# Stick-breaking attention on one core: where the running product over the keys is scanned

## The chip, the core and the metric

The kernel runs on one core of one Trainium2 chip. The metric is device time in microseconds (us), taken over the whole program. Its engines are named as the profile names them: PE (TensorE matmuls), PEld (its weight loads), DVE (VectorE), ACT (ScalarE), POOL (GpSimd) and SP (SyncE, which issues the DMAs).

## What is computed

One layer of a streaming encoder with two token mixers side by side: branch A is a differential softmax attention, branch B a stick-breaking attention. The input is one prompt of 2048 tokens of width 1024 and eight short samples of 16 tokens each with 512 cached keys. Branch B has 8 heads of 64. Cut to branch B, the reference is:

```python
def stick_breaking_attention(q, k, v, qpos, kpos):
    z = einsum('bqhd,bkhd->bhqk', q, k) * (HEAD_DIM_B ** -0.5)
    mask = kpos[None, :] < qpos[:, None]
    log_1m = where(mask, log_sigmoid(-z), 0.0)
    log_a = log_sigmoid(z) + cumsum(log_1m, axis=3, reverse=True) - log_1m
    a = where(mask, exp(log_a), 0.0)
    return einsum('bhqk,bkhd->bqhd', a, v)
```

Without logarithms: the weight of a key is sigmoid(z) of that key times the product of sigmoid(-z) over all later keys. The product over later keys is a running product from the last key to the first, and the kernel computes it with a scan instruction along the keys.

## The kernel before

The work goes by units and query tiles. A unit is one pair of heads of one branch; units 0, 2, 4, 6 are of branch A, units 1, 3, 5, 7 of branch B. In each unit the kernel goes through 16 query tiles of 128 tokens (and one tile with the samples' tokens, first). For each tile it projects queries, keys and values (PE, L428), then scores the tile against all keys up to it, then turns the scores into weights, and two tiles later (`PV_LAG`) multiplies the weights with the values (PE, L700 and L701). Tile t has t+1 blocks of 128 keys, so the last tiles of a unit are the longest. The instruction streams of projection, scores and values are woven into each other by `interleave`, and projections run ahead by about five tiles (`LEAD`), so the last score tiles of a unit stand beside the first projections of the next. Each engine works through its own queue in program order.

For one head of branch B and one tile the steps are these:

- The scores come in chunks of up to 512 keys, each in one PSUM bank of the tag "s", of which there are three. PE writes a chunk with two matmuls (L639, L640), and the last one of a tile gets a mask by a third (L643). Chunks are taken from the last key to the first.
- `evacuate` runs two ACT instructions for each chunk: sigmoid(z) goes to SBUF, into the buffer `sc_p` (L562), and then sigmoid(-z) goes back into the same PSUM bank (L563). Both are recorded under line L119, that of the helper `act`; the masked keys have a score so low that sigmoid(-z) is 1 and sigmoid(z) is 0.
- `stick` scans the chunk on DVE (L616), from its last key to its first, out of PSUM into the SBUF buffer `sc_n`. The second operand is a column of zeros in SBUF, `zero_t`, broadcast along the keys, so that each step computes state times data plus 0. The start value is a constant (2 to the 14th) for the last chunk of all and otherwise the last value of the chunk before, a column of `sc_n`.
- A segment is up to 1024 keys (`SEG` = 8 blocks), and has one buffer `sc_p` and one `sc_n`, six of each. Where a later segment exists, its first column is copied beside the segment's end first (L615).
- When a segment is done, `stick_weights` multiplies sigmoid(z) with the running product of the next key on POOL (L622), both in SBUF. `turn` then splits the weights in a high and a low half in 16 bits: a cast on ACT (L572) and a subtraction on DVE (L573), both from SBUF to SBUF, and SP issues a transposing DMA (L580) that makes the operand `wt` of the value matmuls.

POOL also turns branch A's queries and keys by their positions (L469, L471, L474), multiplies branch B's output with its gate path (L683), and takes part of the splitting of weights (L292). DVE also splits queries, keys and values of the projections (L295, L463) and evacuates branch A's scores (L558).

The samples' scores (`scores_all`, L776 to L781) use the same helpers, with 128 new keys and 512 cached keys in one segment of 640.

Of the kernel before, what the change touches and what calls it, by code (L numbers as in the profile page):

```python
# [20 lines left out]
AF = mybir.ActivationFunctionType  # L21
# [4 lines left out]
P = 128  # L26
# [83 lines left out]
def layer_kernel(ctx: ExitStack, tc: tile.TileContext, a: dict):  # L110
    nc = tc.nc
    V, S, G, T = nc.vector, nc.scalar, nc.gpsimd, nc.tensor
# [4 lines left out]
    def act(**kw):  # L117

        i = S.activation(**kw)  # L119
        if last_table[0] is not None:  # L120
            tc.add_manual_dep(i.ins, last_table[0].ins.name, NOSYNC, reason="table order")
        last_table[0] = i
        return i
# [63 lines left out]
    def bank(tag, dt=F32):  # L187
        return ps.tile([P, 512 if dt == F32 else 1024], dt, tag=tag, name=f"ps_{tag}", bufs=BANKS[tag])
# [16 lines left out]
    zero_t = con.tile([P, 1], F32, name="zero_t")  # L205
# [330 lines left out]
    def new_job(U, t, c, nb, pool=None):  # L536

        segs = [(0, nb)] if t == NT else [(lo, min(lo + SEG, nb)) for lo in range(0, nb, SEG)]
        return dict(U=U, t=t, c=c, pool=pool, segs=[dict(lo=lo, hi=hi) for lo, hi in segs])

    def buffers(job, seg):
        if "p" not in seg:
            for x in "pn":
                if job["t"] == NT:
                    seg[x] = job["pool"].tile([P, 5 * P], F32, tag="dsc", name="dsc", bufs=4)
                else:
                    seg[x] = scp.tile([P, SEG * P + 4], F32, tag=x, name="sc_" + x, bufs=SC_BUFS)

    def evacuate(job, seg, c, p, lo, n, sc_pos, sc_neg, ch):

        buffers(job, seg)
        if job["U"]["kind"] == 0:
            if "mx" not in job:
                job["mx"] = tiny.tile([P, 2, 4], F32, tag="mx", name="mx")
                job["nch"] = 0
            job["nch"] = max(job["nch"], ch + 1)
            dst = seg[("p", "n")[c]]
            V.tensor_scalar(out=dst[:, lo : lo + n], in0=p[:, 0:n], scalar1=sc_pos, scalar2=None,  # L558
                            op0=ALU.mult, op1=ALU.max, accum_out=job["mx"][:, c, ch : ch + 1])
        else:  # L560

            act(out=seg["p"][:, lo : lo + n], in_=p[:, 0:n], func=AF.Sigmoid, scale=sc_pos)  # L562
            act(out=p[:, 0:n], in_=p[:, 0:n], func=AF.Sigmoid, scale=sc_neg)  # L563

    def turn(job, seg, scale=None):

# [36 lines left out]
            V.scalar_tensor_tensor(out=p, in0=n, scalar=r[:, 2:3], in1=p, op0=ALU.mult, op1=ALU.add)  # L603
            turn(job, seg, r[:, 0:1])

    def stick(seg, later, lo, n, src):

        nk = (seg["hi"] - seg["lo"]) * P
        dst = seg["n"]
        if lo + n == nk and later is None:  # L610
            first = 2.0 ** STICK
        else:
            first = dst[:, lo + n : lo + n + 1]
            if lo + n == nk:
                V.tensor_copy(out=first, in_=later["n"][:, 0:1])  # L615
        V.tensor_tensor_scan(out=dst[:, lo : lo + n][:, ::-1], data0=src[:, 0:n][:, ::-1], data1=zero_t[:, 0:1].to_broadcast([P, n]),  # L616
                             initial=first, op0=ALU.mult, op1=ALU.add)

    def stick_weights(job, seg, later):
        m = (seg["hi"] - seg["lo"]) * P - (later is None)  # L620
        p, n = seg["p"], seg["n"]
        G.tensor_tensor(out=p[:, 0:m], in0=p[:, 0:m], in1=n[:, 1 : m + 1], op=ALU.mult)  # L622
        turn(job, seg)

    def scores(U, t, jobs):

        sc, kind = U["sc"], U["kind"]
        nch = t // 4 + 1
        own = [new_job(U, t, c, t + 1) for c in range(1 + kind)]
        jobs += own  # L630

        def chunk(c, ch):
            job = own[c if kind == 1 else 0]
            seg = job["segs"][ch * 4 // SEG]
            n = 512 if ch < t // 4 else (t % 4 + 1) * P
            p = bank("s")
            qst, kk = U["q", t], U["k"][ch]
            diag = ch == t // 4
            T.matmul(p[:, 0:n], qst[:, c, :], kk[:, c, 0:n], start=True, stop=False)  # L639
            T.matmul(p[:, 0:n], qst[:, 2 + c, :], kk[:, c, 0:n], start=False, stop=not diag)  # L640
            if diag:
                m = mask_a if kind == 0 else mask_b
                T.matmul(p[:, n - m.shape[1] : n], idb, m, start=False, stop=True)  # L643
            evacuate(job, seg, c, p, ch * 512 - seg["lo"] * P, n, sc[:, 3:4], sc[:, 4:5], ch)
            if kind == 0:
                if diag and c == 1:
                    softmax_pair(job)
                return
            i = job["segs"].index(seg)
            later = job["segs"][i + 1] if i + 1 < len(job["segs"]) else None  # L650
            stick(seg, later, ch * 512 - seg["lo"] * P, n, p)
            if ch * 4 == seg["lo"]:
                if later is not None:
                    stick_weights(job, later, None)
                if i == 0:
                    stick_weights(job, seg, later)

        def silu():

            z = silu_z[t % len(rings)]  # L660
            sg = stg.tile([P, 256], F32, tag="r2", name="r2", bufs=1)[:, 0:P]
            act(out=sg, in_=z, func=AF.Sigmoid)
            V.tensor_tensor(out=z, in0=z, in1=sg, op=ALU.mult)

        order = [(c, ch) for ch in range(nch) for c in range(2)] if kind == 0 else \
                [(c, ch) for c in range(2) for ch in reversed(range(nch))]
        return ([(0.1, silu)] if kind == 1 else []) + [(2.0 if ch < t // 4 else (t % 4 + 1) / 2, lambda c=c, ch=ch: chunk(c, ch)) for c, ch in order]

    def natural(U, t, po, pool=stg):
# [52 lines left out]
    def sample(U, dec, qpad, cs):  # L722
# [33 lines left out]
        def scores_all():  # L756

            box["jobs"] = [new_job(U, t, c, 5, dec) for c in range(heads)]
            qsam, kn = box["s"][:, 0:4, :], box["s"][:, 4:6, :]
            mask = mask_as if kind == 0 else mask_bs  # L760
            pn = bank("s")
            for c in range(2):
                p = pn[:, c * P : (c + 1) * P]
                T.matmul(p, qsam[:, c, :], kn[:, c, 0:P], start=True, stop=False)
                T.matmul(p, qsam[:, 2 + c, :], kn[:, c, 0:P], start=False, stop=False)
                T.matmul(p, idb, mask, start=False, stop=True)
            for c in range(2):
                pc = bank("s")
                for b in range(2):
                    for f in range(2):  # L770
                        for i in range(4):
                            T.matmul(pc[i * 32 : i * 32 + 32, :], qpad[:, f * 2 + c, 2 * i + b, :], box["k", i][:, b * 4 : b * 4 + 4, c, :],
                                     start=(b == 0 and f == 0), stop=(b == 1 and f == 1))
                job = box["jobs"][c % heads]
                seg = job["segs"][0]
                evacuate(job, seg, c, pn[:, c * P : (c + 1) * P], 512, P, sc[:, 3:4], sc[:, 4:5], 1)  # L776
                evacuate(job, seg, c, pc, 0, 512, box["f"][:, 0:1], box["f"][:, 1:2], 0)
                if kind == 1:
                    stick(seg, None, 512, P, pn[:, c * P : (c + 1) * P])
                    stick(seg, None, 0, 512, pc)  # L780
                    stick_weights(job, seg, None)  # L781
            if kind == 0:
                softmax_pair(box["jobs"][0])
# [39 lines left out]
        steps = [[] for _ in range(13)]  # L823
        steps[4] += [one(queries)]
        steps[6] += [one(scores_all)]
        for i in range(4):
            steps[1 + i] += [one(keys, i)]
# [596 lines left out]
```

## Time and profile before

| what | value |
|---|---|
| median of 3 runs | 2347.12 us (2343.01 to 2352.8) |
| the profiled execution's own time | 2352.01 us |
| its span, from the first to the last instruction | 2350.2 us |
| mean granted TensorE clock in it | 0.965 |

Durations of instructions are those of the profiled execution; its own time is a little above the median of the three runs, and its span is 1.8 us shorter than its time. A row of a group of instructions gives line, engine, operation, the tiles written and read, shape and count, then busy time in us and the mean of one in ns, then the idle time of the engine just before them and who ended it. A row of the timeline gives start and duration in us; rows of the waits give who waited for whom, the sum in us, the count and the longest. `ps_s` is a PSUM bank of scores, `dsc` the samples' buffer in place of `sc_p` and `sc_n`.

### The profile page before, as it was taken

What the parts mean: (1) busy time and instruction counts of PE and PEld (TensorE: products, weight loads), DVE (VectorE), ACT (ScalarE), POOL (GpSimd) and SP (SyncE); (2) the same over time, 40 slices, a digit from 0 to 9 for tenths busy, and PEclk for the clock granted to TensorE, in tenths of its full rate; (3) what the DMA queues carried; (4) which work ended last, traced back from release to release, by engine and by line L of the source; (5) the groups of instructions that cost most, each with busy time, mean ns of one, the idle gap of its engine ahead of it and who ended that gap; (6) DMA issues with size and microseconds to landing.
All of it is one profiled execution on the core that took longest, in us unless ns stands there. A gap on an engine that the chain in (4) does not pass through costs nothing. (4 is left out here: it accounts for less than half of the span.)

```text
span 2350.2 us, 42700 instructions
## 1 busy us (share of the span) xinstructions
PE 2124.9 (90%) x15272; PEld 1144.5 (49%) x15272; DVE 1725.1 (73%) x3652; ACT 1644.4 (70%) x3260; POOL 705.0 (30%) x610
## 2 busy tenths in 40 slices
PE   5898899998999999899999979998996879988998
PEld 3554454444555445445545545554553344544443
DVE  4848866779875667978667797877688877777663
ACT  4557878787886778878677777866777656665541
POOL 1533012446300334731033474103335111221111
PEclk8999899999999999999999999999996989999999
DMA  9766759887895988867577787766687999999531
GB/s 334 252 203 177 165 127 263 180 188 163 207 227 131 213 199 189 175 175 191 139 188 175 186 171 185 192 146 149 142 175 162 288 238 250 237 249 243 157 103 48
DMA packets 834357, 445.34 MB, mean 189 GB/s; under 512 B 537210, under 2 KB 777130, under 8 KB 833632
## 3 DMA queue, kind: packets, MB, share of 16 engines
q1 hardware_dynamic: 833196, 442.24, 76.5%
q8 instruction: 119, 1.95, 0.3%
q14 instruction: 94, 0.77, 0.1%
q10 hardware_dynamic: 948, 0.39, 0.1%
HBM read 245.60 MB, written 69.24 MB: 134 GB/s over the span
## 5 line engine op out<-in xcount | busy, mean ns | idle before, releaser
L622 POOL TENSOR_TENSOR sc_p<-sc_p,sc_n 128x127 f32<-128x127 f32 (+7 forms) x192 | 314.2, 1640 | 834.8 <-DVE sc_n L616 812.5
L428 PE MATMUL ps_mm<-wb,hs 128*128 128x512 f16 x1632 | 412.1, 380 | 5.1 <-DMA hs<-hT_d 3.0
L428 PEld LDWEIGHTS <-hs 128*128 128x128 f16 x3120 | 275.8, 99 | 264.5 <-issue 14.8
L428 PE MATMUL ps_mm<-wa,hs 128*128 128x512 f16 x1488 | 377.7, 384 | 9.0 <-DVE qbuf L463 3.8
L616 DVE TENSOR_TENSOR_SCAN sc_n<-ps_s,sc_n,zero_t 128x512 f32<-128x512 f32 x192 | 245.5, 1279 | 80.8 <-ACT ps_s L119 77.5
L639 PE MATMUL ps_s<-k,qst 128*128 128x512 f16 (+3 forms) x640 | 227.5, 356 | 37.2 <-DVE sc_n L616 25.8
L573 DVE TENSOR_TENSOR sc_n<-sc_p,sc_n 128x128 f16<-128x128 f32 (+7 forms) x192 | 211.5, 1106 | 51.8 <-ACT sc_n L572 51.3
L504 PEld LDWEIGHTS <-hs 128*128 128x128 f16 x1632 | 155.6, 98 | 181.4 <-DVE qst L532 5.5
L119 ACT ACTIVATE sc_p<-ps_s,usc 128x512 f32<-128x512 f32 (+3 forms) x320 | 204.3, 638 | 35.3 <-PE ps_s L640 27.9
L640 PE MATMUL ps_s<-k,qst 128*128 128x512 f16 (+3 forms) x640 | 227.1, 356 | 0.0
L572 ACT CAST sc_n<-sc_p 128x128 f16<-128x128 f32 (+7 forms) x192 | 154.9, 811 | 78.9 <-POOL sc_p L622 76.0
L700 PE MATMUL ps_o<-v,wt 128*128 128x128 f16 x1088 | 172.2, 226 | 35.1 <-DMA wt<-sc_n 35.1
L119 ACT ACTIVATE ps_s<-ps_s,usc 128x512 f32<-128x512 f32 (+3 forms) x328 | 199.4, 608 | 0.0
L504 PE MATMUL ps_t<-wb,hs 128*128 128x512 f16 x816 | 192.9, 380 | 2.5 <-DVE qst L532 2.2
L504 PE MATMUL ps_t<-wa,hs 128*128 128x512 f16 x816 | 192.3, 381 | 3.1 <-DVE qst L532 2.2
L1341 PE MATMUL ps_o<-wo,wb 128*128 128x512 f16 x816 | 189.2, 386 | 4.0 <-ACT wb L1163 4.0
L701 PE MATMUL ps_o<-v,wt 128*128 128x64 f16 x1088 | 158.3, 198 | 0.0
L700 PEld LDWEIGHTS <-wt 128*128 128x128 f16 x1088 | 105.6, 101 | 100.1 <-DMA wt<-sc_n 46.4
L558 DVE TENSOR_SCALAR_CACHE_REDUCE sc_n<-ps_s,usc 128x512 f32<-128x512 f32 (+3 forms) x160 | 106.5, 666 | 42.2 <-PE ps_s L640 22.9
L616 DVE TENSOR_TENSOR_SCAN sc_n<-ps_s,zero_t 128x128 f32<-128x128 f32 (+3 forms) x128 | 104.2, 815 | 41.0 <-ACT ps_s L119 38.0
L558 DVE TENSOR_SCALAR_CACHE_REDUCE sc_p<-ps_s,usc 128x512 f32<-128x512 f32 (+3 forms) x160 | 106.4, 665 | 35.6 <-PE ps_s L640 26.1
L701 PEld LDWEIGHTS <-wt 128*128 128x128 f16 x1088 | 103.4, 101 | 54.5 <-issue 1.9
(358 smaller groups left out, 4531.3 us busy)
## 6 DMA issues: line engine op xcount, KB each, us to landing
hs<-hT_d SPq DMA_DIRECT2D x130, 512.0 KB, 4.4
g_d<-gt SPq DMA_DIRECT2D x68, 256.0 KB, 4.4
wb<-g_d SPq DMA_DIRECT2D x26, 512.0 KB, 5.7
out_dram<-pr SPq DMA_DIRECT2D x204, 64.0 KB, 2.4
o_d<-o SPq DMA_DIRECT2D x136, 64.0 KB, 2.0
hs<-o_d SPq DMA_DIRECT2D x17, 512.0 KB, 5.1
out_dram<-x SPq DMA_DIRECT2D x17, 512.0 KB, 2.8
wide<-in_w_ada_dram SPq DMA_DIRECT2D x8, 1024.0 KB, 7.8
```

Source lines behind the costliest of these rows:

```text
L119: i = S.activation(**kw)
L428: T.matmul(box["p"], box["h"][:, hi, k, :], U["w"][k][:, wi, :], start=(n == 0), stop=(n == 3 * KT - 1))
L504: T.matmul(box["g"][:, 0:gw], box["h"][:, hi, k, :], U["wg"][k // per][:, k % per, wi, :], start=(j == 0), stop=(j == 3 * KT - 1))
L558: V.tensor_scalar(out=dst[:, lo : lo + n], in0=p[:, 0:n], scalar1=sc_pos, scalar2=None, op0=ALU.mult, op1=ALU.max, accum_out=job["mx"][:, ...
L573: V.tensor_tensor(out=lo, in0=src, in1=hi, op=ALU.subtract)
L616: V.tensor_tensor_scan(out=dst[:, lo : lo + n][:, ::-1], data0=src[:, 0:n][:, ::-1], data1=zero_t[:, 0:1].to_broadcast([P, n]), initial=fi ...
L622: G.tensor_tensor(out=p[:, 0:m], in0=p[:, 0:m], in1=n[:, 1 : m + 1], op=ALU.mult)
L639: T.matmul(p[:, 0:n], qst[:, c, :], kk[:, c, 0:n], start=True, stop=False)
L640: T.matmul(p[:, 0:n], qst[:, 2 + c, :], kk[:, c, 0:n], start=False, stop=not diag)
L700: T.matmul(po[:, c * P : (c + 1) * P], wt[:, wj, :], vt[:, c, :, :], start=first, stop=False)
L701: T.matmul(po[:, c * P : c * P + 64], wt[:, nb + wj, :], vt[:, c, 0, :], start=False, stop=last)
L1341: T.matmul(po, st["y"][:, yi * 8 + k, :], wo[j * 4 + k // 2][:, wi, k % 2, :], start=(n == 0), stop=(n == 3 * KT - 1))
```

## The change

sigmoid(-z) is written to SBUF, into `sc_n`, instead of back into the PSUM bank, and it is written before sigmoid(z). The scan no longer follows each chunk: it runs once for a whole segment, in place in `sc_n`, when the segment's last chunk (the one with its first keys) has been evacuated. For the samples the two scans of 128 and 512 keys become one of 640. The copy of the later segment's first column, the multiplication on POOL and all that follows stay.

```diff
@@ evacuate
+            act(out=seg["n"][:, lo : lo + n], in_=p[:, 0:n], func=AF.Sigmoid, scale=sc_neg)
             act(out=seg["p"][:, lo : lo + n], in_=p[:, 0:n], func=AF.Sigmoid, scale=sc_pos)
-            act(out=p[:, 0:n], in_=p[:, 0:n], func=AF.Sigmoid, scale=sc_neg)
@@ stick
-    def stick(seg, later, lo, n, src):
+    def stick(seg, later, lo, n):
...
-        V.tensor_tensor_scan(out=dst[:, lo : lo + n][:, ::-1], data0=src[:, 0:n][:, ::-1], data1=zero_t[:, 0:1].to_broadcast([P, n]),
+        x = dst[:, lo : lo + n][:, ::-1]
+        V.tensor_tensor_scan(out=x, data0=x, data1=zero_t[:, 0:1].to_broadcast([P, n]),
                              initial=first, op0=ALU.mult, op1=ALU.add)
@@ scores, chunk
-            stick(seg, later, ch * 512 - seg["lo"] * P, n, p)
             if ch * 4 == seg["lo"]:
+                stick(seg, later, 0, (seg["hi"] - seg["lo"]) * P)
                 if later is not None:
                     stick_weights(job, later, None)
@@ sample, scores_all
-                    stick(seg, None, 512, P, pn[:, c * P : (c + 1) * P])
-                    stick(seg, None, 0, 512, pc)
+                    stick(seg, None, 0, 5 * P)
                     stick_weights(job, seg, None)
```

## The prediction, made before the changed kernel was run

> **What bounds the kernel now.** I read the page's busy shares first, then busy time by stretch of 50 us, then the scan line by itself, then waits and timeline where the stretches differ.
>
> ```profile
> span 2350.2 us, 42700 instructions
> PE 2124.9 (90%) x15272; PEld 1144.5 (49%) x15272; DVE 1725.1 (73%) x3652; ACT 1644.4 (70%) x3260; POOL 705.0 (30%) x610
> 850.00:900.00 50.00, 49.10 (x318) 25.24 (x316) 38.94 (x59) 37.35 (x74) 19.54 (x14) 1.00 0.69 154
> 500.00:550.00 50.00, 41.45 (x320) 22.19 (x319) 45.89 (x54) 43.41 (x80) 33.73 (x25) 1.00 0.93 186
> 950.00:1000.00 50.00, 42.05 (x373) 24.01 (x371) 48.74 (x75) 38.62 (x77) 34.37 (x27) 0.97 0.88 168
> 1350.00:1400.00 50.00, 39.73 (x340) 22.33 (x340) 48.25 (x50) 41.25 (x78) 37.08 (x27) 1.00 0.86 185
> 1750.00:1800.00 50.00, 33.26 (x291) 19.43 (x289) 46.18 (x57) 41.06 (x72) 29.54 (x17) 0.76 0.82 166
> sum 200.00, PE 156.49 PEld 87.95 DVE 189.06 ACT 164.35 POOL 134.71; mean PE 39.12 PEld 21.99 DVE 47.26 ACT 41.09 POOL 33.68
> ```
>
> The columns of a stretch are length, then PE, PEld, DVE, ACT and POOL busy, granted clock, DMA share, GB/s. The whole kernel is PE's (90%), and so is the middle of a branch-B unit: 49.10 of 50 us in 850:900, with DVE at 38.94. The four last stretches, one at the end of each branch-B unit, differ: DVE has 189.06 of 200 us, PE only 156.49. There the last, longest query tiles meet the next unit's first projections, and DVE sets the pace. So the change is decided by what it does to DVE in these four places; elsewhere DVE has room.
>
> How much of DVE is scan, by shape, and what stands beside it:
>
> ```profile
> L616 DVE TENSOR_TENSOR_SCAN sc_n<-ps_s,sc_n,zero_t 128x512 f32<-128x512 f32 x192 | 245.5, 1279 | 80.8 <-ACT ps_s L119 77.5
> L616 DVE TENSOR_TENSOR_SCAN sc_n<-ps_s,zero_t 128x512 f32<-128x512 f32 x32 | 38.9, 1215 | 9.4 <-ACT ps_s L119 8.3 <-DMA wb<-in_cache_b_k_dram 1.1
> L616 DVE TENSOR_TENSOR_SCAN sc_n<-ps_s,zero_t 128x384 f32<-128x384 f32 x32 | 30.4, 950 | 12.9 <-ACT ps_s L119 11.7 <-PE ps_s L643 1.2
> L616 DVE TENSOR_TENSOR_SCAN sc_n<-ps_s,zero_t 128x256 f32<-128x256 f32 x32 | 21.9, 683 | 14.1 <-ACT ps_s L119 13.5 <-PE ps_t L521 0.4
> L616 DVE TENSOR_TENSOR_SCAN sc_n<-ps_s,zero_t 128x128 f32<-128x128 f32 x32 | 13.1, 411 | 4.6 <-ACT ps_s L119 4.5
> L616 DVE TENSOR_TENSOR_SCAN sc_n<-ps_s,sc_n,zero_t x192: 1265/1282/1285, 353.5 to 1801.2; 128x512 f32<-128x512 f32 x192
> L573 DVE TENSOR_TENSOR sc_n<-sc_p,sc_n x192: 266/1093/3052, 331.5 to 1808.3; 128x1024 f16<-128x1024 f32 x80, 128x128 f16<-128x128 f32 x16, 128x256 f16<-128x256 f32 x16, 128x384 f16<-128x384 f32 x16
> ```
>
> Of line and durations (minimum/median/maximum in ns): 192 scans of one shape all lie between 1265 and 1285. The subtraction L573, whose two inputs are both in SBUF, goes to 3052. The timeline of one tail says why:
>
> ```profile
> 965.79 2.96 POOL L622 TENSOR_TENSOR sc_p<-sc_p,sc_n 128x1024 f32<-128x1024 f32 x1 [1.42 <-DVE sc_n L616]
> 965.81 1.08 DVE L573 TENSOR_TENSOR sc_n<-sc_p,sc_n 128x896 f16<-128x896 f32 x1
> 969.85 1.99 POOL L622 TENSOR_TENSOR sc_p<-sc_p,sc_n 128x1023 f32<-128x1023 f32 x1 [1.10 <-DVE sc_n L616]
> 970.13 1.27 DVE L616 TENSOR_TENSOR_SCAN sc_n<-ps_s,sc_n,zero_t 128x512 f32<-128x512 f32 x1
> 979.87 1.99 POOL L622 TENSOR_TENSOR sc_p<-sc_p,sc_n 128x1023 f32<-128x1023 f32 x1
> 980.04 2.90 DVE L573 TENSOR_TENSOR sc_n<-sc_p,sc_n 128x1024 f16<-128x1024 f32 x1
> 991.23 1.22 DVE L573 TENSOR_TENSOR sc_n<-sc_p,sc_n 128x1024 f16<-128x1024 f32 x1
> ```
>
> L573 started at 980.04 under a POOL multiplication that ended at 981.86; its 2.90 us are 1.82 of waiting and 1.08 of its own, less than the 1.22 it takes alone. Started just after DVE, at 965.8, it is POOL that waits: 2.96 instead of 1.99. So POOL and a DVE instruction with both inputs in SBUF take turns, whole instruction by whole instruction. The scan at 970.13 lay wholly inside a POOL multiplication and kept its 1.27: its data came from PSUM.
>
> **The change, part by part.** *Scan time.* The slope of the shapes is (1215-411)/384 = 2.09 ns a key, the fixed part 411-128x2.09 = 143 ns, and 1279-1215 = 64 ns more when the start value is a column. For 1024 keys in one go that makes 2.14+0.14 = 2.29 us, against 1.22+1.28 = 2.49 for two halves. All scans of the prompt take 245.5+38.9+30.4+21.9+13.1 = 349.8 us. They are 320; in one go per segment they are 192 (one for each of 64 head-tiles up to tile 7, two for each of 64 from tile 8 on). The 128 that go are all continuations that start from a column, and each takes its fixed 143+64 = 207 ns with it: 26.5 us, which leaves 323.3. No row has a scan out of SBUF. I take the slope of PSUM: the subtraction reads two streams from SBUF in 1.08 us for 896 keys, 1.2 ns a key, so SBUF is not what would hold a scan to 2.09. On the fixed part I allow 0.05 us either way, 10 us over 192 scans.
>
> *The price of the new place.* data0 now lies in SBUF, data1 (the zero column) did already: the scan becomes an instruction with two SBUF inputs, of the kind of L573 and no longer of the kind that POOL cannot touch. It takes turns with POOL. The four tails, line by line (the sum of L616, then L573 tail by tail with its sum, then L622):
>
> ```profile
> sum 200.00, DVE 89.55; mean DVE 22.39
> 500.00:550.00 50.00, 15.75 (x9) 1.00 0.93 186
> 950.00:1000.00 50.00, 15.73 (x9) 0.97 0.88 168
> 1350.00:1400.00 50.00, 20.05 (x9) 1.00 0.86 185
> 1750.00:1800.00 50.00, 13.59 (x12) 0.76 0.82 166
> sum 200.00, DVE 65.12; mean DVE 16.28
> 500.00:550.00 50.00, 20.71 (x10) 1.00 0.93 186
> 950.00:1000.00 50.00, 15.45 (x7) 0.97 0.88 168
> 1350.00:1400.00 50.00, 20.94 (x10) 1.00 0.86 185
> 1750.00:1800.00 50.00, 26.66 (x12) 0.76 0.82 166
> sum 200.00, POOL 83.77; mean POOL 20.94
> ```
>
> L573 has 9+9+9+12 = 39 instructions, at most 39x1.22 = 47.6 us of own work in its 65.12; 17.5 are waits for POOL. L622 has 10+7+10+12 = 39, at most 39x1.99 = 77.6. POOL's other work is 134.71-83.77 = 50.9, some of it waiting too; with L573's share of waiting (17.5 of 65.1) taken off, 37. The turn-takers of the four tails after the change: scans 89.55x323/350 = 82.7, subtractions 47.6, multiplications 77.6, other POOL work 37: 245 us, in 200 us. So if they are packed without a gap the tails grow by 45 us. At the other end DVE and POOL never overlap at all: DVE's remaining 189.06-89.55-65.12 = 34.4, less the same share, adds 25, so +70. Outside the tails I look at the late parts of the units as a whole (400:565, 825:1005, 1240:1410, 1650:1810; total, then L616, then L622):
>
> ```profile
> sum 675.00, PE 607.38 PEld 325.67 DVE 547.73 ACT 526.69 POOL 327.85; mean PE 151.85 PEld 81.42 DVE 136.93 ACT 131.67 POOL 81.96
> sum 675.00, DVE 278.19; mean DVE 69.55
> sum 675.00, POOL 250.39; mean POOL 62.60
> ```
>
> At 2.5 us for 1024 keys, 278.19 us is 111 such pieces: scans 257, multiplications 111x1.99 = 221, subtractions 111x1.22 = 135, other POOL work (327.85-250.39)x0.73 = 57: 670 us of turns in 675. Less the tails' 245 that is 425 in 475: nearly full, but it fits, and DVE has (675-547.73)-(200-189.06) = 116 us of idle time there to wait in. I add between nothing and a tenth of that, 12 us. Together +45 to +82, and I take the middle, +64: in a tail nearly every DVE instruction before or after a POOL one takes turns, yet the projection's PSUM reads still overlap.
>
> The Trainium skill (SBUF — State Buffer, section "Who interferes with whom") states this as a rule: a Vector instruction with two SBUF inputs and a GpSimd instruction that reads SBUF share one read interface, the one that starts first keeps it throughout and the other blocks fully, while with at most one SBUF input there is no contention. By it the broadcast column counts as an input, and the sum is the one above; the trace agrees for the subtraction (2.90 us), and no row shows a broadcast second input.
>
> *What is freed.* A score bank is free after the second sigmoid, no longer after the scan:
>
> ```profile
> PE ps_s L639 <- DVE sc_n L616: 25.8, 35, 2.1
> PE ps_o L700 <- DMA wt<-sc_n: 35.1, 24, 5.2
> L119 ACT ACTIVATE sc_p<-ps_s,usc 128x512 f32<-128x512 f32 x224 | 157.6, 703 | 31.8 <-PE ps_s L640 27.9 <-PE ps_s L643 3.4
> L119 ACT ACTIVATE ps_s<-ps_s,usc 128x512 f32<-128x512 f32 x224 | 152.1, 679 | 0.0
> ```
>
> The wait of 25.8 us (35 times) ends. I credit nothing: in the tails PE would then wait for DVE's product instead, through the weights (the 35.1 us of the second row), since DVE is what runs out. If DVE had room, 25.8 would be the gain.
>
> *The rest.* sigmoid(-z) written to SBUF costs ACT as sigmoid(z) does, 703 instead of 679 ns: 24 ns, some 8 us in 320, hidden since ACT has 41.09 of 50 us in the tails; uncovered it would be 2 us a unit. The two sigmoids change places, which lets the last chunk's scan start 0.7 us earlier; the scan as a whole starts only when the segment's last chunk is through, so its end moves by up to 2.29-1.28 = 1 us. Behind a waiting scan stand, on DVE, the subtractions and the next unit's key and query splits, for which PE's transposes wait. No DMA is added or taken; SP issues the weight transposes as late as the cast comes. Two tiles of lag cover 1 us. The sample tiles' eight scan pairs save some 0.2 us each, off the path: 0.
>
> **The rivals.** *Faster: the zero column takes no turn.* It is one element, read again and again; if it is held inside DVE, the scan has one streamed SBUF input and stays untouched by POOL. Then DVE loses 27 us, in the tails 89.55-82.7 = 7, and the 25.8 us of bank waits go: 7 to 33 us, say 22 less: 2325. For it: no row shows a broadcast input waiting. Against: it is a second operand like any other, as in L573. It decides if the 1024-key scans keep to 2.3 us beside POOL.
>
> *No change: turns fall into idle time.* DVE idles 675-547.73 = 127 us in the late stretches. If the tails' surplus moves ahead of or behind them, the 670 us of turns fit into 675: 2347, no change. Against: PE's order is fixed and the weights lag two tiles only, so a tail cannot borrow from the middle.
>
> *Worse than the sum.* PE, starved, also ran at a granted clock of 0.76 in 1750:1800; if each tail does so and full turns spread into the middle, 82 us and half as much again, 2347+123 = 2470 or more.
>
> **How the numbers follow.** The profiled execution took 2352.0 us (span 2350.2), 5 us above the median 2347.1 of the three runs; the sum is added to the median: 2347+64 = 2411. Chances: forecast 0.74, zero column free 0.14, idle time 0.07, worse 0.05. The range leaves out the first and the last rival: 2343 to 2480. Half a per cent, 12 us, is about what a measurement here can tell from no change: faster 0.14, same 0.07, slower 0.79.
>
> **What would show it.** Right: 192 scans, 80 of them of 1024 keys (64 with a column start), whose shortest are near 2.29 and 2.35 us and whose longest near 2.35+1.99 = 4.3; POOL's 1024-key multiplications well above their mean now; DVE full and PE below 39 of 50 us in the tails; PE's wait for the scan gone and that for weights longer. Wrong: 1024-key scans all within some 20 ns of 2.29 or 2.35 us, or stretched scans while the tails keep their length.

## The result, and the profile after

| | before | after |
|---|---|---|
| median | 2346.73 us (4 runs) | 2420.32 us (4 runs, 2417.38 to 2424.82) |
| ratio, 95% interval | 1 | 1.0313 [1.0285, 1.034] |
| the profiled execution's own time | 2352.01 us | 2417.38 us |
| its span | 2350.2 us | 2415.6 us |
| mean granted clock in it | 0.965 | 0.956 |

The change costs 73.6 us by the medians, 65.4 us by the two profiled spans. The forecast was 64 us slower.

The head of the page after, to be held against the same two lines before:

```profile
span 2415.6 us, 42571 instructions
PE 2142.0 (89%) x15272; PEld 1154.6 (48%) x15272; DVE 1796.9 (74%) x3516; ACT 1645.7 (68%) x3260; POOL 788.7 (33%) x610
```

DVE has 136 instructions fewer (128 scans of the prompt and 8 of the samples) and is busy 71.8 us longer. POOL has the same 610 instructions and is busy 83.7 us longer. Nobody gave these engines more work; they wait inside their instructions. The rows of lines show it, first the scan with minimum, median and maximum, then the groups with sum and mean, all of the kernel after (its line numbers are one higher from here on):

```profile
L617 DVE TENSOR_TENSOR_SCAN sc_n<-sc_n,zero_t x192: 397/2277/4080, 328.6 to 1868.9; 128x1024 f32<-128x1024 f32 x80, 128x128 f32<-128x128 f32 x16, 128x256 f32<-128x256 f32 x16, 128x384 f32<-128x384 f32 x16
L617 DVE TENSOR_TENSOR_SCAN sc_n<-sc_n,zero_t 128x128 f32<-128x128 f32 (+7 forms) x192 | 378.2, 1975 | 76.2 <-ACT sc_n L119 74.5 <-DMA out_dram<-pr 0.5
L617 DVE TENSOR_TENSOR_SCAN sc_n<-sc_n,zero_t 128x1024 f32<-128x1024 f32 x80 | 212.0, 2651 | 33.4 <-ACT sc_n L119 32.9
L623 POOL TENSOR_TENSOR sc_p<-sc_p,sc_n 128x1024 f32<-128x1024 f32 x64 | 148.4, 2319 | 183.4 <-DVE sc_n L617 133.2 <-ACT sc_p L119 21.0 <-ACT sc_n L119 8.6
L573 DVE TENSOR_TENSOR sc_n<-sc_p,sc_n 128x1024 f16<-128x1024 f32 x80 | 130.7, 1634 | 23.0 <-ACT sc_n L572 23.0
```

The same groups of the multiplication and the subtraction before:

```profile
L622 POOL TENSOR_TENSOR sc_p<-sc_p,sc_n 128x1024 f32<-128x1024 f32 x64 | 139.8, 2184 | 215.2 <-DVE sc_n L616 207.5 <-DVE sc_e L223 2.9 <-DVE gt L663 2.7
L573 DVE TENSOR_TENSOR sc_n<-sc_p,sc_n 128x1024 f16<-128x1024 f32 x80 | 120.6, 1508 | 32.9 <-ACT sc_n L572 32.6
```

There are 192 scans, 80 of them of 1024 keys. They take 378.2 us, where 320 scans took 349.8 us before and the forecast's own work for 192 was 323. The longest is 4080 ns; before, the 192 scans of one shape lay within 20 ns of each other. The long multiplications and subtractions took turns before too and grew by a tenth or less (2184 to 2319 ns, 1508 to 1634). More than half of POOL's growth is in its other work: the two products of the positions (L469 and L471) take 143.5 us and took 116.9, the gate product (L683 before, L684 after) 64.3 and took 41.3.

How the time is lost shows in one chain in the timeline, ahead of the end of unit 3 (start, duration):

```profile
962.23 2.81 DVE L617 TENSOR_TENSOR_SCAN sc_n<-sc_n,zero_t 128x1024 f32<-128x1024 f32 x1
962.85 3.52 POOL L623 TENSOR_TENSOR sc_p<-sc_p,sc_n 128x767 f32<-128x767 f32 x1
966.34 0.72 POOL L474 TENSOR_TENSOR rot<-rot,r 128x256 f32<-128x256 f32 x1
967.02 2.00 POOL L623 TENSOR_TENSOR sc_p<-sc_p,sc_n 128x1024 f32<-128x1024 f32 x1
967.27 2.56 DVE L573 TENSOR_TENSOR sc_n<-sc_p,sc_n 128x768 f16<-128x768 f32 x1 [1.99 <-ACT sc_n L572]
970.22 0.34 DVE L295 SCALAR_TENSOR_TENSOR k<-rot,sq,k 128x128 f16<-128x128 f32 x1
970.61 0.39 PE L517 MATMUL ps_t<-id,k 128*128 128x128 f16 x2 [3.70 <-DVE k L295]
997.53 3.03 POOL L623 TENSOR_TENSOR sc_p<-sc_p,sc_n 128x1023 f32<-128x1023 f32 x1 [2.70 <-DVE sc_n L617]
998.88 3.82 DVE L617 TENSOR_TENSOR_SCAN sc_n<-sc_n,zero_t 128x1024 f32<-128x1024 f32 x1
```

The multiplication that POOL begins at 962.85 stands still until the scan ends at 965.04 and is through at 966.37. POOL's last step on the next unit's queries and keys (L474) comes late by that. The subtraction at 967.27 then stands still under POOL's next multiplication, which ends at 969.02. The split of the keys is behind it on DVE, and PE's transpose of those keys has waited 3.70 us. The last two rows are the other way round: the scan of 998.88 waits for a multiplication that ends at 1000.56 and then needs its own 2.1 us or so.

What PE waits for, in the waits of the kernel after (sum in us, times, longest):

```profile
PE ps_o L701 <- DMA wt<-sc_n: 58.3, 26, 6.8
PE ps_t L517 <- DVE k L295: 26.5, 9, 5.9
PE ps_s L640 <- ACT sc_p L119: 14.0, 10, 2.8
PE ps_t L517 <- DVE sc_n L615: 12.1, 3, 5.1
```

The row of 25.8 us for the scan's end is gone, and in its place there is one of 14.0 us for the second sigmoid. The wait for weights has grown from 35.1 to 58.3. The wait for the split of the keys is new among the large ones; the kernel before has it so:

```profile
PE ps_t L517 <- DVE k L295: 12.1, 11, 2.0
```

The last row of the kernel after is of the same transposes; there the profile names a copy on DVE as what ended the wait. Before it had no such row. By these rows the transposes of the keys waited 12.1 us for DVE and now wait 38.6, the largest growth of all.

Where in the program the time went: busy time by stretch, with the stretches cut at the same tiles in both kernels. First the four branch-B units from their first scan to the first scan of tile 12, then from there to the unit's last scan, then the 50 us that end with it. The sums of the kernel before:

```profile
sum 596.30, PE 564.25 PEld 294.76 DVE 419.13 ACT 451.87 POOL 211.32; mean PE 141.06 PEld 73.69 DVE 104.78 ACT 112.97 POOL 52.83
sum 322.50, PE 271.56 PEld 149.25 DVE 279.50 ACT 261.97 POOL 187.77; mean PE 67.89 PEld 37.31 DVE 69.87 ACT 65.49 POOL 46.94
sum 200.00, PE 152.95 PEld 87.41 DVE 193.16 ACT 165.17 POOL 138.78; mean PE 38.24 PEld 21.85 DVE 48.29 ACT 41.29 POOL 34.69
```

And of the kernel after:

```profile
sum 627.60, PE 580.75 PEld 301.19 DVE 463.65 ACT 455.30 POOL 239.57; mean PE 145.19 PEld 75.30 DVE 115.91 ACT 113.83 POOL 59.89
sum 359.20, PE 273.79 PEld 150.96 DVE 309.01 ACT 257.56 POOL 240.25; mean PE 68.45 PEld 37.74 DVE 77.25 ACT 64.39 POOL 60.06
sum 200.00, PE 131.41 PEld 75.11 DVE 183.08 ACT 143.29 POOL 155.27; mean PE 32.85 PEld 18.78 DVE 45.77 ACT 35.82 POOL 38.82
```

The branch-B units took 596.3 + 322.5 = 918.8 us and now take 986.8: 68.0 more, all of the span's growth. Of it 36.7 us lie in tiles 12 to 15 and 31.3 us before. In the last 50 us of a unit PE fell from 38.2 to 32.9 us busy, and DVE and POOL together have 338 us busy in 200, as against 332, with fewer of their instructions done (148 and 85 against 216 and 100).

### The profile page after: what moved, and what is told of

Its sections match the earlier page's. It is cut to its first block, busy times and chain, and to the rows that moved or that the text cites. A ratio compares the mean times of both kernels' runs of the same rounds, so it can differ in the third digit from the quotient of the medians.

```text
span 2415.6 us, 42571 instructions
## 1 busy us (share of the span) xinstructions
PE 2142.0 (89%) x15272; PEld 1154.6 (48%) x15272; DVE 1796.9 (74%) x3516; ACT 1645.7 (68%) x3260; POOL 788.7 (33%) x610
## 5 line engine op out<-in xcount | busy, mean ns | idle before, releaser
L623 POOL TENSOR_TENSOR sc_p<-sc_p,sc_n 128x127 f32<-128x127 f32 (+7 forms) x192 | 348.9, 1822 | 800.8 <-DVE sc_n L617 447.8
L617 DVE TENSOR_TENSOR_SCAN sc_n<-sc_n,zero_t 128x128 f32<-128x128 f32 (+7 forms) x192 | 378.2, 1975 | 76.2 <-ACT sc_n L119 74.5
L428 PE MATMUL ps_mm<-wb,hs 128*128 128x512 f16 x1632 | 419.5, 387 | 1.3 <-DMA hs<-hT_d 1.1
L428 PEld LDWEIGHTS <-hs 128*128 128x128 f16 x3120 | 277.2, 100 | 256.7 <-issue 17.9
L428 PE MATMUL ps_mm<-wa,hs 128*128 128x512 f16 x1488 | 379.1, 387 | 4.5 <-DVE v L295 2.4
L573 DVE TENSOR_TENSOR sc_n<-sc_p,sc_n 128x128 f16<-128x128 f32 (+7 forms) x192 | 229.1, 1201 | 71.2 <-ACT sc_n L572 71.0
L640 PE MATMUL ps_s<-k,qst 128*128 128x512 f16 (+3 forms) x640 | 230.1, 360 | 26.5 <-ACT sc_p L119 14.0
L701 PE MATMUL ps_o<-v,wt 128*128 128x128 f16 x1088 | 178.3, 228 | 61.4 <-DMA wt<-sc_n 58.3
L119 ACT ACTIVATE sc_n<-ps_s,usc 128x512 f32<-128x512 f32 (+3 forms) x320 | 203.8, 637 | 24.0 <-PE ps_s L641 14.2
L469 POOL TENSOR_TENSOR rot<-pr,rope 128x256 f32<-128x256 f32 x68 | 74.4, 1094 | 194.1 <-ACT pr L442 132.1
L558 DVE TENSOR_SCALAR_CACHE_REDUCE sc_p<-ps_s,usc 128x512 f32<-128x512 f32 (+3 forms) x160 | 106.5, 666 | 38.8 <-PE ps_s L641 31.3
```

The lines of the kernel that those rows point to most:

```text
L428: T.matmul(box["p"], box["h"][:, hi, k, :], U["w"][k][:, wi, :], start=(n == 0), stop=(n == 3 * KT - 1))
L573: V.tensor_tensor(out=lo, in0=src, in1=hi, op=ALU.subtract)
L617: V.tensor_tensor_scan(out=x, data0=x, data1=zero_t[:, 0:1].to_broadcast([P, n]), initial=first, op0=ALU.mult, op1=ALU.add)
L701: T.matmul(po[:, c * P : (c + 1) * P], wt[:, wj, :], vt[:, c, :, :], start=first, stop=False)
```

## The experiments

Each ratio is to the kernel before, run beside it on the same chip. Two theories stood against each other from the start. *Turns*: the scan now has both inputs in SBUF, so it and POOL's instructions stop each other. *Delay*: the scan begins only when the whole segment has been evacuated, so all that follows comes later.

### Undoing the merge alone

The kernel after, with every chunk scanned as soon as it is written, still in SBUF.

```diff
+            stick(seg, later, ch * 512 - seg["lo"] * P, n)
             if ch * 4 == seg["lo"]:
-                stick(seg, later, 0, (seg["hi"] - seg["lo"]) * P)
```

> The changed kernel, but each chunk of up to 512 keys is scanned as soon as it is written, as in the kernel before; only the place stays changed (SBUF instead of PSUM). Turn theory (a scan with both inputs in SBUF takes turns with POOL): the scans wait as in the changed kernel and there are 128 more of them, 26 us more scan work: 2425 to 2455 us, scans of 512 keys between 1.2 and 3.3 us. Delay theory (the loss comes from scanning only when the whole segment is there): the delay is gone, 2335 to 2360 us.

Measured: 2441.8 us, ratio 1.0375 [1.0358, 1.0392]. The group of its 512-key scans:

```profile
L617 DVE TENSOR_TENSOR_SCAN sc_n<-sc_n,zero_t 128x512 f32<-128x512 f32 x224 | 358.3, 1601 | 59.7 <-ACT sc_n L119 50.4 <-DMA wa<-in_cache_a_k_dram 1.3 <-ACT sc_n L572 0.5
```

The delay is gone and the time is not back, so delay falls as the cause of the loss. The scans, 1215 and 1279 ns for this shape out of PSUM, have a mean of 1601. Against the kernel after (1.0313) the merge itself gives 0.6%, some 15 us; the 26.5 us of scan work that it saves are worth something here, where the turns make each instruction on DVE dear.

### The zero column in PSUM, with two score banks

If turns are the cause, the scan must go free when its second input leaves SBUF. The kernel's four tags hold eight PSUM banks (2, 3, 1 and 2). Here the column takes one of the three score banks. Two controls have the same two score banks: the kernel after and the kernel before.

```diff
-    BANKS = {"mm": 2, "s": 3, "t": 1, "o": 2}
+    BANKS = {"mm": 2, "s": 2, "t": 1, "o": 2, "z": 1}
...
-    zero_t = con.tile([P, 1], F32, name="zero_t")
-    V.memset(zero_t, 0.0)
+    zero_t = bank("z")
+    V.memset(zero_t[:, 0:1], 0.0)
```

> The changed kernel with two score banks, and the zero column of the scan in the PSUM bank that this frees: the scan is as late and as long as in the changed kernel, but has one input in SBUF and one in PSUM. Turn theory: scans of 1024 keys all within 0.05 us of 2.28, and 60 to 100 us less than the control, 2320 to 2360 us. Delay theory: as the control within 10 us. If the zero column takes no turn at all (the rival of the prediction): as the control too, and its scans as stretched as there.

The control of the kernel after and that of the kernel before differ from their kernels in this line only:

```diff
-    BANKS = {"mm": 2, "s": 3, "t": 1, "o": 2}
+    BANKS = {"mm": 2, "s": 2, "t": 1, "o": 2}
```

> Control for the next run: the changed kernel with two score banks instead of three. Both theories: close to the changed kernel, 2415 to 2440 us, since a bank is free as soon as ACT has read it twice.

> Control: the kernel before with two score banks instead of three. There a bank is held until the scan is through, so PE's 25.8 us of waits for the scan should grow: 2355 to 2400 us by both theories. What it lies above the kernel before is what the early release of the bank can be worth when banks are short.

Measured: column in PSUM 2495.33 us, 1.0596 [1.0572, 1.062]; after with two banks 2534.11, 1.0765 [1.0733, 1.0798]; before with two banks 2536.92, 1.0775 [1.0755, 1.0795]. The scan with the column in PSUM, then its 1024-key group:

```profile
L617 DVE TENSOR_TENSOR_SCAN sc_n<-sc_n,ps_z x192: 394/1880/2349, 343.6 to 1932.3; 128x1024 f32<-128x1024 f32 x80, 128x128 f32<-128x128 f32 x16, 128x256 f32<-128x256 f32 x16, 128x384 f32<-128x384 f32 x16
L617 DVE TENSOR_TENSOR_SCAN sc_n<-sc_n,ps_z 128x1024 f32<-128x1024 f32 x80 | 186.3, 2329 | 32.0 <-ACT sc_n L119 31.8
```

The scans went free as expected: with the column in PSUM the maximum is 2349 ns, with it in SBUF 4080. But the times of all three runs missed what was expected of them. The column's move gave 38.8 us and not 60 to 100. I had expected the loss of a score bank to cost some tens of us, and it costs the kernel before 184 (2536.92 against 2352.63). So the 39 us are taken from a kernel that is short of banks, and another place for the column had to be found. In this setting the whole change costs nothing that can be told (2534.11 against 2536.92): what the turns take, the rest of the change gives back.

### The zero column in PSUM, with three score banks

Here the column takes one of the two banks of the value sums, and the sums of the first and the last stage, which used those too, go into the score banks.

```diff
-    BANKS = {"mm": 2, "s": 3, "t": 1, "o": 2}
+    BANKS = {"mm": 2, "s": 3, "t": 1, "o": 1, "z": 1}
...
-    zero_t = con.tile([P, 1], F32, name="zero_t")
-    V.memset(zero_t, 0.0)
+    zero_t = bank("z")
+    V.memset(zero_t[:, 0:1], 0.0)
...
-                pt = bank("so"[k % 2])
+                pt = bank("s")
...
-                po = bank("o")
+                po = bank("s")
```

> The same with the zero column in the PSUM bank that this frees: the scan keeps its time and length and has one input in SBUF and one in PSUM. PE, ACT, POOL and SP have the order of the control. Turn theory: scans unstretched (1024 keys within 0.05 us of 2.28 or 2.35) and 60 to 100 us less than the control. With two score banks the same edit gave 39 us, in a kernel that was short of banks elsewhere. If the loss of the changed kernel is mostly something else (the later scan, or the order in which the engines take their work): less than 40 us below the control.

The two controls, of the kernel after and of the kernel before:

```diff
-    BANKS = {"mm": 2, "s": 3, "t": 1, "o": 2}
+    BANKS = {"mm": 2, "s": 3, "t": 1, "o": 1}
...
-                pt = bank("so"[k % 2])
+                pt = bank("s")
...
-                po = bank("o")
+                po = bank("s")
```

> Control for the next run: the changed kernel with one bank for the value sums instead of two (and the last stage's output sums in the score banks). The three score banks stay. A tile's value sum must be read out before the next one begins; I estimate up to 1 us for each of 128 tiles, partly covered. 2420 to 2500 us by both theories.

> The kernel before with one bank for the value sums. Turn theory: the control lies above this by about what the change cost (50 to 90 us), and the run with the zero column in PSUM lies at this or up to 50 us below it (26 us less scan work, banks released early). If the order or the delay matters, that run lies above this one instead.

Measured: column in PSUM 2386.29 us, 1.0151 [1.0117, 1.0185]; after 2450.28, 1.0433 [1.0417, 1.0449]; before 2380.86, 1.0123 [1.0099, 1.0148]. The kernel after with one value bank, in head, 1024-key scans, and sum of the stretches from tile 12 to the last scan:

```profile
span 2448.8 us, 42566 instructions
PE 2144.6 (88%) x15272; PEld 1158.1 (47%) x15272; DVE 1799.5 (73%) x3516; ACT 1646.6 (67%) x3260; POOL 796.7 (33%) x610
L617 DVE TENSOR_TENSOR_SCAN sc_n<-sc_n,zero_t 128x1024 f32<-128x1024 f32 x80 | 219.8, 2748 | 54.0 <-ACT sc_n L119 53.4
sum 350.70, PE 273.36 PEld 154.99 DVE 298.89 ACT 257.64 POOL 242.24; mean PE 68.34 PEld 38.75 DVE 74.72 ACT 64.41 POOL 60.56
```

The same with the column in PSUM, with the group of all its prompt scans as well:

```profile
span 2372.4 us, 42566 instructions
PE 2125.6 (90%) x15272; PEld 1150.4 (48%) x15272; DVE 1744.5 (74%) x3516; ACT 1644.7 (69%) x3260; POOL 706.1 (30%) x610
L617 DVE TENSOR_TENSOR_SCAN sc_n<-sc_n,ps_z 128x128 f32<-128x128 f32 (+7 forms) x192 | 321.1, 1678 | 126.6 <-ACT sc_n L119 125.7
L617 DVE TENSOR_TENSOR_SCAN sc_n<-sc_n,ps_z 128x1024 f32<-128x1024 f32 x80 | 186.4, 2330 | 54.6 <-ACT sc_n L119 54.0
sum 309.30, PE 267.80 PEld 149.95 DVE 278.00 ACT 259.22 POOL 190.17; mean PE 66.95 PEld 37.49 DVE 69.50 ACT 64.80 POOL 47.54
```

This is the cleanest pair of the study: the two traces have the same instructions in the same order on every engine, and the programs differ only in the place of one column. It is worth 2450.28 - 2386.29 = 64.0 us of the 2450.28 - 2380.86 = 69.4 us that the change costs in this setting. POOL's busy time falls by 90.6 us and DVE's by 55. POOL's multiplications of 1024 keys have no part in that (a mean of 2314 ns with the column in SBUF, 2324 with it in PSUM); its shorter multiplications and its other products have. What is left, 5.4 us, is within the intervals of the two ratios.

### Merging without turns

The same kernel, column in PSUM and three score banks, but scanned chunk by chunk.

```diff
+            stick(seg, later, ch * 512 - seg["lo"] * P, n)
             if ch * 4 == seg["lo"]:
-                stick(seg, later, 0, (seg["hi"] - seg["lo"]) * P)
```

> The changed kernel with the zero column in PSUM (one bank for the value sums), but scanned chunk by chunk again: no turns with POOL, 128 more scans (26 us of DVE work), the banks still released by ACT. Against the run with whole segments (2386 us, 1.015 of before) it measures what one scan for a whole segment is worth when no turns are in the way. If DVE's scan time sets the pace in the tails: 5 to 25 us more, 2390 to 2412 us. If the later start of the scan costs as much as its shorter time gives: the same within 8 us.

Measured: 2382.78 us, 1.0127 [1.0089, 1.0165], as against 1.0151 [1.0117, 1.0185] in one go. Without turns one scan for a segment is worth nothing that these runs can tell, and nor is the early release of the bank, for both are level with the kernel before in the same banks (1.0123).

### Without POOL's multiplication

If the turns are taken mostly with the multiplication, the change must cost far less where it is not done. In both kernels the multiplication of branch B is replaced by a copy of one column, so the weights lack the factor of the later keys.

```diff
-        G.tensor_tensor(out=p[:, 0:m], in0=p[:, 0:m], in1=n[:, 1 : m + 1], op=ALU.mult)
+        G.tensor_copy(out=p[:, 0:1], in_=n[:, 1:2])
```

> The kernel before without branch B's multiplication on POOL (the weights are then sigmoid(z) alone; a one-column copy keeps the order of the steps). POOL keeps little to take turns with. Both theories: the subtractions lose their waits, 10 to 40 us less than before, 2310 to 2340 us.

> The changed kernel without that multiplication. Turn theory: the scans have little left to wait for, so it lies within 25 us of the run before it, 1024-key scans close to 2.3 us on average (2.65 in the changed kernel). Any theory in which the changed place or time of the scan costs by itself, POOL or no POOL: 50 to 80 us above the run before it.

Measured: before without it 2331.58 us, 0.9901 [0.9867, 0.9934]; after without it 2360.54, 1.0031 [1.001, 1.0051]. The groups of the kernel after without the multiplication:

```profile
L617 DVE TENSOR_TENSOR_SCAN sc_n<-sc_n,zero_t 128x1024 f32<-128x1024 f32 x80 | 191.6, 2397 | 60.3 <-ACT sc_n L119 59.4 <-DMA wb<-in_w_in_dram 0.6
L573 DVE TENSOR_TENSOR sc_n<-sc_p,sc_n 128x1024 f16<-128x1024 f32 x80 | 98.8, 1236 | 44.4 <-ACT sc_n L572 44.4
```

The scan is nearly back at its own 2330, the subtraction is wholly so, and the price of the change falls from 73.6 to 29 us. That is a little above the 25 expected, a difference that the intervals of the two ratios cover. The mean of 2397 says that some turns with POOL's other work are left; (2397 - 2330) x 80 is 5 us of DVE. The rest of the 29 us is not settled: the instructions stand in another order on several engines in the two kernels, and no run here holds that order while it takes the multiplication out.

### Moving the subtraction to POOL

The kernel before has turns of its own, between the subtraction (L573) and POOL. If DVE's own busy time sets the pace of the tails, taking subtractions off DVE makes it faster; if the turns do, it gives nothing, since POOL is slower at it and takes the turn all the same. In the first kernel the second head's subtraction goes to POOL in tiles 12 to 15, in the second in all tiles.

```diff
-            V.tensor_tensor(out=lo, in0=src, in1=hi, op=ALU.subtract)
+            (G if job["c"] == 1 and 12 <= job["t"] < NT else V).tensor_tensor(out=lo, in0=src, in1=hi, op=ALU.subtract)
```

> A version of the kernel before: in the query tiles 12 to 15 the subtraction of the second head goes to POOL instead of DVE. In the tails DVE has 47 of 50 us and POOL 34; a piece of 1024 keys takes some 2 us on POOL and 1.2 to 1.6 on DVE with its waits. If DVE's own work sets the tails' pace, it loses some 30 us of 189 there: 2320 to 2345 us. If the turns set it, POOL's longer instruction takes away what DVE gains: 2340 to 2365 us.

```diff
-            V.tensor_tensor(out=lo, in0=src, in1=hi, op=ALU.subtract)
+            (G if job["c"] == 1 and job["t"] < NT else V).tensor_tensor(out=lo, in0=src, in1=hi, op=ALU.subtract)
```

> The same for the second head in all query tiles. Outside the tails PE sets the pace, so it should differ from the run before it by less than 10 us; in the tails the same bounds hold, 2320 to 2365 us in all.

Measured: last tiles alone 2361.29 us, 1.0043 [1.0025, 1.006]; all tiles 2386.11, 1.0137 [1.012, 1.0154]. A group of the first:

```profile
L573 POOL TENSOR_TENSOR sc_n<-sc_p,sc_n 128x1024 f16<-128x1024 f32 x20 | 44.6, 2235 | 2.9 <-ACT sc_n L572 2.9
```

On POOL it has a mean of 2235 ns, waits included, where DVE alone takes 1236. In the tails, 32 instructions less on DVE gained nothing. That fits DVE and POOL being one resource there, but does not prove it, for the subtraction itself also takes longer there. The second kernel missed: I expected it within some 10 us of the first, because ahead of tile 12 I still thought DVE and POOL had room, and it lost another 25. The prediction's term for the earlier tiles rests on the same thought.

No kernel that computes everything beat the kernel before.

## Why the prediction was right, and where not

**The mechanism.** Right, and shown by the pair of equal programs: a broadcast column of one element in SBUF counts as the second SBUF input for the whole length of the scan, and its place alone decides 64 of the 69 us. That is also the rule of the Trainium skill that the prediction weighed (SBUF — State Buffer, "Who interferes with whom"): two SBUF inputs contend with a GpSimd instruction that reads SBUF, at most one does not, outside the 2-port performance modes. It leaves open what a broadcast input does, and the runs fill that in (a maximum of 4080 ns with two SBUF inputs, 2349 with one). The rival "the zero column takes no turn" falls by the 4080 ns of the longest scan, and by 2349 ns with the column in PSUM. With the column there, the time is that of the kernel before in the same banks, not the 22 us less that the rival promised.

**Scan time.** 323.3 us of own work were forecast, from the slope of scans out of PSUM; the 192 scans out of SBUF that POOL cannot touch take 321.1. The saving is real (28.7 us by these sums), and worth nothing that the runs can tell without turns and some 15 us with them. The 2.29 us for 1024 keys is 2.28 by the prediction's own slope and fixed part.

**The tails.** Forecast +45 to +70. The sum was made for the 200 us of four fixed stretches; tiles 12 to 15, which hold them but for the last 14 us of the second, grew by 36.7. The term that was too high is the packing of all turns into those four stretches. The tiles are not bound to them, and waiting also fell ahead of tile 12; how much moved, and how much of the 45 was never there, no run separates. PE's idle time in these tiles grew from 50.9 to 85.4 us, and the path was only in part the one forecast, through the weights. That holds in the last of the four units, where PE's wait for them went from 11.7 to 23.4 us. In the three others it is the transposes of the next unit's keys, behind the split on DVE: summed over the three, 12.0 us before, and 26.3 with another 12.1 of the copy's row after. The prediction names these splits and gives them no price.

**The earlier tiles.** Forecast 0 to +12, measured +31.3. The step that failed is the one that put the wait into DVE's idle time. DVE did have it, and in the earlier tiles it is still busy only 463.65 of 627.6 us. But PE waits for one result, not for DVE's mean. By the sums of these tiles PE is idle 46.9 us where it was 32.1. The most of that growth is PE's wait for weights, here unit by unit, first before, then after:

```profile
PE ps_o L700 <- DMA wt<-sc_n: 3.7, 3, 2.8
PE ps_o L700 <- DMA wt<-sc_n: 3.3, 3, 2.1
PE ps_o L700 <- DMA wt<-sc_n: 1.2, 2, 0.8
PE ps_o L700 <- DMA wt<-sc_n: 3.0, 2, 1.7
PE ps_o L701 <- DMA wt<-sc_n: 5.6, 4, 2.7
PE ps_o L701 <- DMA wt<-sc_n: 5.9, 3, 2.8
PE ps_o L701 <- DMA wt<-sc_n: 5.4, 3, 2.9
PE ps_o L701 <- DMA wt<-sc_n: 3.1, 2, 2.7
```

That is 11.2 us before and 20.0 after. Scan, multiplication, cast, subtraction and transposing DMA follow one another to make these weights, so a wait inside any of them can make them late, however long DVE idles elsewhere; which of them did is not separated. The split of the keys, which costs PE most in tiles 12 to 15, ends no wait of PE that the profile lists here. PE is also busy 16.5 us longer. These stretches hold 3817 matmuls now and held 3761, and 56 at 0.15 us are some 8 us of work that moved in; the rest are slightly longer matmuls (the granted clock is 0.98 to 0.99 and was 0.97 to 1.00), which no run explains.

The two errors, about 20 us too much in the tails and 25 too little before, nearly cancel: that the total came out nearer than its parts is luck.

**The bank.** Credited with nothing, and rightly: the wait of 25.8 us went and the kernel gained nothing, in the setting without turns too. With two score banks the credit is probably not nothing: there the column in PSUM is 42 us below the kernel before (2495.33 against 2536.92), whose wait for the scan is longer. No run separates the bank's part of the 42 from that of the fewer scans:

```profile
PE ps_s L639 <- DVE sc_n L616: 38.5, 37, 3.5
```

**The signs.** 192 scans, 80 of 1024 keys, the longest near 4.3 us (4.08), PE below 39 of 50 us in the tails (32.9, by stretches in which it had 38.2 before), the waits for the scan gone and for weights longer: all there. POOL's long multiplications rose, but little (2184 to 2319 ns), and as the pair of equal programs has them alike, they are no sign of the scan's turns. One was wrong in three units of four: DVE is not full in their last 50 us (44.0, 44.2 and 45.3, in the last unit 49.6). There it also waits outside its instructions, most of it for the cast (5.1, 5.1 and 3.1 us), which follows POOL's product. "Turns fall into idle time" fails by the tails' length. "Worse than the sum" did not come, though one part of it did: the granted clock, below.

**What stays open.** The 5.4 us between the column in PSUM and the kernel before in the same banks, which may be nothing, and the part of the 29 us without multiplication that is not turns.

## What to carry to other kernels

Before an operand of VectorE moves from PSUM to SBUF, count the instruction's inputs that are then in SBUF, the broadcast ones too, and look at what GpSimd does beside it: minimum, median and maximum of its line tell at a glance whether it takes turns. A constant that is needed for every step of a long scan is worth a place in PSUM if one is free; if that place costs a bank that the matmuls use, price the bank first. Saving fixed costs on an engine that has room gives nothing, and idle time in the mean is no cushion when another engine waits for the next result.

## What the runs showed that I had not expected

- The third score bank: without it the kernel before needs 184 us more (2536.92 against 2352.63), although its wait for the scan grew only from 25.8 to 38.5 us. Other waits of PE grew more: for `hs` (L428) from 4.5 to 47.3 us, for weights (L700) from 35.1 to 55.0, for branch A's evacuations (L639) from 10.9 to 39.3.
- A scan of 1024 keys out of SBUF and in place takes 2330 ns in the mean with its zeros in PSUM, as the slope of scans out of PSUM had said; the place of the data does not change its speed, only who can stop it.
- PE's busy time moves with the granted clock: 2124.9 us at 0.965 before, 2142.0 at 0.956 after, with the same 15272 matmuls; the products, 2051 and 2048, are alike. So of the 65.4 us of span, 17 are PE running slower and 48 are PE idle. In the last 50 us of the four units, where PE has least to do, the clock is lower after than before (the figure behind the last count of each row; before, in the same four places, 0.97, 0.99, 1.00 and 0.74):

```profile
526.00:576.00 50.00, 37.66 (x305) 21.69 (x306) 44.04 (x38) 37.27 (x70) 41.19 (x24) 0.86 0.69 150
966.00:1016.00 50.00, 37.23 (x316) 21.88 (x314) 44.18 (x39) 37.27 (x70) 41.21 (x24) 0.90 0.68 150
1404.00:1454.00 50.00, 35.68 (x296) 20.05 (x294) 45.28 (x40) 36.59 (x69) 41.29 (x23) 0.93 0.69 149
1823.00:1873.00 50.00, 20.84 (x163) 11.49 (x163) 49.57 (x31) 32.15 (x51) 31.58 (x14) 0.67 0.51 99
```

That a starved PE is also granted less is read from these rows together, not from a run made for it.
